# Ordering the engines of a two-layer encoder trunk by a simulation with timelines

## The chip, the core and the metric

The kernel runs on one core of one Trainium2 chip, as one program. The metric is device time in microseconds (us) for one execution; a time without a unit below is in microseconds.

## What is computed

Two layers of an encoder over 256 positions of width 1024, in float32. Each layer is a half step of a gated feed-forward network (FFN, inner width 2816), a mixer, and a second FFN half step:

```
for l in range(DEPTH):
    h_res = h_res + 0.5 * swiglu(rmsnorm(h_res, ffn1_norm[l]), ffn1_w_gate[l], ffn1_w_up[l], ffn1_w_down[l])
    z = rmsnorm(h_res, mix_norm[l]) @ w_in[l]
    zq, zk, zv, zp, hq, hi, hff, hfb, hg = jnp.split(z, split_idx, axis=-1)
    y_att = dilated_attention(zq, zk, zv, q_norm[l], k_norm[l], biases)
    y_pool = pool_mixer(zp, pool_w[l], pool_scale[l])
    y_rec = hgrn2_bidirectional(hq, hi, hff, hfb, hg, lb_all[0, l], lb_all[1, l], hgrn_norm[l])
    h_res = h_res + jnp.concatenate([y_att, y_pool, y_rec], axis=-1) @ w_out[l]
    h_res = h_res + 0.5 * swiglu(rmsnorm(h_res, ffn2_norm[l]), ffn2_w_gate[l], ffn2_w_up[l], ffn2_w_down[l])
```

The attention mixes three dilations, the pooling takes means over windows of 2 to 16, and the recurrence (HGRN2) runs in both directions.

## The kernel before, in words

Every product of float32 matrices is made of three matmuls in the fp32r form: each operand is split into a high part, which is the value rounded by a copy on ScalarE (ACT), and a low part, which is the rest, by a subtraction on VectorE (DVE). TensorE (PE) then adds high by high, high by low and low by high into one PSUM bank (lines 174 to 176, or 167 to 169 where the weights are the stationary operand).

The weights come as a list of 328 halves of 128 x 1024 values in the order of use. SyncE (SP) issues their loads (line 133), four buffers deep. Line 149 makes `whi` of a half on ACT, line 151 makes `wlo` on DVE, or on GpSimd (POOL) for 35 halves of the mixers. Five buffers of each hold what is ready ahead of PE.

The program has six stages: FFN, mixer, FFN in each layer.

- An FFN stage runs over 11 blocks of 256 inner columns. `gate_up` makes 48 matmuls of 512 columns into two `gu` banks; line 345 (ACT, Silu) and line 346 (DVE) make the block's `h`; `turn` transposes it (`hp`, line 352, four transposes) and line 259 (ACT) and line 260 (DVE) split it into `hi` and `lo`; `down` makes 24 matmuls into four `ya` banks, which add up over all blocks. The transposes of a block are traced in the middle of the `down` of the block before.
- A mixer stage projects into `ga`, `gb`, `hq`, `q`, `k`, `zh`, `hg`, `v`, and runs the three head groups between these projections, in the order of a string (`ORDER`). The recurrence goes by levels 0, 1, 2, 4 up to 128: for each level DVE multiplies `U` and `W` (line 520), PE makes a group of small `lev` matmuls (line 541; 549 and 553 for the last two), and DVE or ACT copies the result into place (line 566 and others). The output projection goes to four `wo` banks.
- Between two stages the residual `x` is brought up to date and transposed. There are five such boundaries. The last block's `down` is traced with a hook behind each of the four accumulators:

```
    def add(self, y, by, dh, tt, post):
        s = self.x[:, tt, dh * 512:dh * 512 + 512]
        self.nc.vector.scalar_tensor_tensor(s, y, by, s, op0=ALU.mult, op1=ALU.add)
        post(dh, tt)
```

The add is line 371 (DVE). The hook (`to_stage`) calls `squares` (line 283, ACT, sums of squares for the norm; behind the fourth one an ACT table load, line 287, where the stage needs it) and `turn` (line 296, PE, four transposes into `xps`). When both position halves of a group are there, `parts` makes `xh` (line 274, ACT) and `xl` (line 275, DVE), the split operand of the next stage, in eight pieces numbered k = 0 to 7. One `xps` bank holds two pieces.

The PSUM pool `pg` has four banks, and `gu`, `hp`, `xps`, `ga`, `gb` and most of the mixer's results take turns in them (`self.pg = pool("pg", 4, space=PSUM)`); `py` has four more, for `ya`, `wo` and `lev`. So the first bank that a new stage needs comes free when both pieces of an `xps` bank have been read by line 274 and by line 275.

At the start x comes in transposed, in four pieces (line 114), and as it is (line 119, 1 MB, on ACT's queue). The first weight half is split in two parts, and ACT has in this order: `whi` of the first part, `xh` of pieces 0 and 1, `whi` of the second part, `xh` of pieces 2 to 7, two whole `whi`, the four squares, the table load.

**What sets the order.** The kernel is written with a tile layer. Its scheduler takes the traced operations with their dependencies, a priority by place in the trace, and a simulation of the machine, and writes for each engine a fixed list of instructions with semaphore waits. On the chip each engine goes through its list in that order. SP alone is left in traced order (`manual_schedule`). `keep_in_program_order` and `issue_after` (lines 287, 307, 395) tie a few ACT instructions to others.

## Time and profile before

| | |
|---|---|
| three runs | 1040.72, 1041.35, 1043.30; median 1041.35 |
| the profiled execution | 1040.81, of which 1039.0 is the span of the instructions |
| mean granted PE clock over the span | 0.993 of full speed |
| PE busy | 1004.4 (97%) |
| DVE, ACT, POOL busy | 585.0, 538.8, 88.3 |
| HBM read | 180.2 MB, 176 GB/s over the span |

The profile is of one execution, recorded in hardware. A busy time is the union of an engine's instructions; PE's matmuls overlap each other, since one begins before the one ahead of it has drained, so an idle time of PE below is what is left between the drained and the next. The granted clock is 1.0 where PE runs at 2.4 GHz and 0.5 where it runs at 1.2 GHz. A wait is put down to the instruction whose semaphore came last.

### The profile page before, as it was taken

The numbers are of one execution on the slowest core, as the hardware profiler recorded it, in microseconds if no ns is written. First come the engines' busy times: TensorE is split into PE (matmuls) and PEld (weight loads), VectorE is DVE, ScalarE is ACT, GpSimd is POOL, SyncE is SP. The second block draws the span as 40 slices with busy tenths as digits, with TensorE's granted clock in tenths as the row PEclk, the third lists the DMA queues.
The fourth block names the chain that finished last, engine by engine and source line by source line (L and its number), as shares of the span: only waits on it lengthen the run. The fifth ranks groups of instructions, "written<-read, shape, count | busy, mean of one in ns | idle before, by whom it ended". The sixth has DMA issues, their size and how long they took to land.

```text
span 1039.0 us, 14421 instructions
## 1 busy us (share of the span) xinstructions
PE 1004.4 (97%) x5682; PEld 826.2 (80%) x5682; DVE 585.0 (56%) x776; ACT 538.8 (52%) x774; POOL 88.3 (8%) x43
## 2 busy tenths in 40 slices
PE   6999999998999999999999999999889999999998
PEld 4878888886867888888878888889768678888886
DVE  5655555669835555555565555554977155555553
ACT  7544444684865544444564444447648555444442
POOL 0000000140230000000000000004132400000000
PEclk9999999999999999999999999999989999999999
DMA  7769655553334555555555555554523346555551
GB/s 265 245 219 329 234 188 193 165 163 123 103 122 136 179 192 182 186 192 188 185 168 187 190 185 186 195 185 138 165 83 102 102 147 196 184 185 189 194 186 58
DMA packets 50420, 182.20 MB, mean 175 GB/s; under 512 B 5768, under 2 KB 6024, under 8 KB 49968
## 3 DMA queue, kind: packets, MB, share of 16 engines
q1 hardware_dynamic: 48528, 174.09, 51.6%
q0 software_dynamic: 720, 4.21, 1.1%
q10 hardware_dynamic: 1104, 2.99, 0.8%
q8 instruction: 44, 0.72, 0.3%
q14 instruction: 24, 0.20, 0.1%
HBM read 180.20 MB, written 3.16 MB: 176 GB/s over the span
## 4 chain that ended last, share of the span: by engine, by line
PE 87%; DVE 6%; ACT 3%; issue 3%; DMA 1%; POOL 0%; SPq 0%; ACTq 0%; DVEq 0%; POOLq 0%
PE gu L175 15%; PE gu L176 15%; PE gu L174 15%; PE ya L174 8%; PE ya L176 8%; PE ya L175 8%; PE hp L352 2%; PE wo L174 2%; PE wo L175 1%; PE wo L176 1%; ACT whi L149 1%; DVE wlo L151 1%; PE xps L296 1%; DMA bias<-x_t 1%; PE lev L541 1%
## 5 line engine op out<-in xcount | busy, mean ns | idle before, releaser
L149 ACT ACTIVATE whi<-stage 128x1024 fp32r<-128x1024 f32 (+1 forms) x329 | 347.1, 1056 | 395.3 <-PE gu L176 202.3
L151 DVE TENSOR_TENSOR wlo<-stage,whi 128x1024 fp32r<-128x1024 f32 (+1 forms) x294 | 360.7, 1229 | 337.5 <-ACT whi L149 337.4
L174 PE MATMUL gu<-whi,xh 128*128 128x512 f32 x704 | 275.7, 392 | 8.0 <-ACT xh L274 5.7
L175 PE MATMUL gu<-wlo,xh 128*128 128x512 f32 x704 | 274.9, 391 | 0.5 <-DVE wlo L151 0.5
L176 PE MATMUL gu<-whi,xl 128*128 128x512 f32 x704 | 274.7, 390 | 0.0
L174 PEld LDWEIGHTS gu<-whi,xh 128*128 128x128 f32 x704 | 132.5, 188 | 37.5 <-ACT xh L274 5.7
L175 PEld LDWEIGHTS gu<-wlo,xh 128*128 128x128 f32 x704 | 132.7, 189 | 28.7 <-DVE wlo L151 1.4
L176 PEld LDWEIGHTS gu<-whi,xl 128*128 128x128 f32 x704 | 132.6, 188 | 27.7
L174 PE MATMUL ya<-whi,hi 128*128 128x512 f32 x352 | 141.2, 401 | 0.0
L151 POOL TENSOR_TENSOR wlo<-stage,whi 128x1024 fp32r<-128x1024 f32 x35 | 85.0, 2437 | 654.5 <-ACT whi L149 639.2
L176 PE MATMUL ya<-whi,lo 128*128 128x512 f32 x352 | 137.8, 391 | 0.0
L175 PE MATMUL ya<-wlo,hi 128*128 128x512 f32 x352 | 137.4, 390 | 0.0
L176 PEld LDWEIGHTS ya<-whi,lo 128*128 128x128 f32 x352 | 66.1, 188 | 14.3
L175 PEld LDWEIGHTS ya<-wlo,hi 128*128 128x128 f32 x352 | 66.3, 188 | 12.4
L174 PEld LDWEIGHTS ya<-whi,hi 128*128 128x128 f32 x352 | 66.2, 188 | 12.3
L345 ACT ACTIVATE g<-gu,rc 128x256 f32<-128x256 f32 x88 | 41.5, 475 | 47.4 <-PE gu L176 47.4
L346 DVE SCALAR_TENSOR_TENSOR h<-gu,rc,g 128x256 f32<-128x256 f32 x88 | 42.0, 481 | 23.7 <-ACT g L345 23.7
L260 DVE TENSOR_TENSOR lo<-hp,hi 128x512 fp32r<-128x512 f32 x44 | 30.1, 684 | 2.8 <-ACT hi L259 2.8
L259 ACT ACTIVATE hi<-hp 128x512 fp32r<-128x512 f32 x44 | 25.6, 581 | 2.7 <-PE hp L352 2.7
L541 PE MATMUL lev<-U,W 64*64 64x64 f32 x384 | 15.6, 237 | 11.4 <-DVE W L520 11.4
L352 PEld LDWEIGHTS hp<-cst,h 128*128 128x128 f32 x176 | 21.8, 139 | 5.7
L352 PE MATMUL hp<-cst,h 128*128 128x128 f32 x176 | 26.3, 272 | 0.0
(224 smaller groups left out, 1035.8 us busy)
## 6 DMA issues: line engine op xcount, KB each, us to landing
stage<-w_all SPq DMA_DIRECT2D x327, 512.0 KB, 3.5
skew<-drow POOLq DMA_DIRECT2D x1, 2048.0 KB, 12.1
bias<-skew POOLq DMA_DIRECT2D x2, 1024.0 KB, 10.3
bias<-x_t SPq DMA_DIRECT2D x4, 256.0 KB, 7.9
x<-x ACTq DMA_DIRECT2D x1, 1024.0 KB, 8.4
band<-band ACTq DMA_DIRECT2D x1, 1024.0 KB, 8.0
y_t<-x SPq DMA_DIRECT2D x4, 256.0 KB, 2.2
stage<-w_all SPq DMA_DIRECT2D x2, 256.0 KB, 4.7
```

Of the source, the lines that this page charges most:

```text
L149: nc.scalar.activation(hi[:, s], st[:, s], AF.Copy)
L151: eng.tensor_tensor(lo[:, s], st[:, s], hi[:, s].bitcast(F32), op=ALU.subtract)
L174: nc.tensor.matmul(out, lhsT=ah, rhs=wh, start=start, stop=False, skip_group_check=True)
L175: nc.tensor.matmul(out, lhsT=ah, rhs=wl, start=False, stop=False, skip_group_check=True)
L176: nc.tensor.matmul(out, lhsT=al, rhs=wh, start=False, stop=stop, skip_group_check=True)
L259: self.nc.scalar.activation(hi, src, AF.Copy)
L260: self.nc.vector.tensor_tensor(lo, src, hi.bitcast(F32), op=ALU.subtract)
L296: nc.tensor.transpose(self.xps[k // 2][:, j % 2, tt * P:tt * P + P], self.x[:, tt, k * P:k * P + P], self.ident)
L345: silu = nc.scalar.activation(g2[:, tt, :], gu[tt][:, 0:256], AF.Silu, scale=r)
L346: nc.vector.scalar_tensor_tensor(h[:, tt, :], gu[tt][:, 256:512], r, g2[:, tt, :], op0=ALU.mult, op1=ALU.mult)
L352: nc.tensor.transpose(hp[:, f, tt * P:tt * P + P], h[:, tt, f * P:f * P + P], self.ident)
L541: nc.tensor.matmul(ps[d][e * 64:e * 64 + 64, hb * 64:hb * 64 + 64], lhsT=a, rhs=c, start=(hb == 0), stop=(hb == 7), skip_group_check=True)
```

## The change

One argument is given to the tile layer. Its scheduler then orders the instructions by another simulation of the machine, one that keeps a timeline for each engine, in place of the one it used; the traced operations, their dependencies, the buffers and the kernel's text are otherwise the same.

```diff
-    with tile.TileContext(nc) as tc:
+    with tile.TileContext(nc, schedule_with_timeline_sim=True) as tc:
         trunk_kernel(tc, *args)
```

The lists of PE, DVE and ACT change all through the program; those of SP and POOL stand as they were. No instruction is added or taken away. Three places follow, each as the list stood and as it stands now (line, operation, output and inputs, shape of the output, how many in a row).

**ACT at the start.** `whi` is a weight half's high part, `xh` the split input, `sq` the squares of x, `rc` the norm's factor. Before:

```order
L149 ACTIVATE whi<-stage 128x512
L274 ACTIVATE xh<-bias,prm 128x256 x2
L149 ACTIVATE whi<-stage 128x512
L274 ACTIVATE xh<-bias,prm 128x256 x6
L149 ACTIVATE whi<-stage 128x1024 x2
L283 ACTIVATE sq,ss<-x 128x512 x4
L287 ACT_TABLE_LOAD
```

Now:

```order
L149 ACTIVATE whi<-stage 128x512
L274 ACTIVATE xh<-bias,prm 128x256 x2
L283 ACTIVATE sq,ss<-x 128x512 x4
L287 ACT_TABLE_LOAD
L149 ACTIVATE whi<-stage 128x512
L274 ACTIVATE xh<-bias,prm 128x256 x4
L307 ACTIVATE rc<-rc,cols 128x2
L274 ACTIVATE xh<-bias,prm 128x256 x2
L149 ACTIVATE whi<-stage 128x1024 x2
```

The four squares and the table load now stand ahead of the second part of the first weight half, of six of the eight pieces and of the first whole half.

**PE at the boundary between the layers** (the last `down` of layer 0, then the first `gate_up` of layer 1). `ya` are the four accumulators of `down`, `xps` the transposes of x, `gu` the next stage's first products. Before, the end of it:

```order
L174 MATMUL ya<-whi,hi 128x512
L296 MATMUL xps<-cst,x 128x128 x4
L175 MATMUL ya<-wlo,hi 128x512
L176 MATMUL ya<-whi,lo 128x512
L296 MATMUL xps<-cst,x 128x128 x4
L174 MATMUL gu<-whi,xh 128x512
```

Now:

```order
L176 MATMUL ya<-whi,lo 128x512 x2
L174 MATMUL ya<-whi,hi 128x512
L175 MATMUL ya<-wlo,hi 128x512
L176 MATMUL ya<-whi,lo 128x512
L296 MATMUL xps<-cst,x 128x128 x16
L174 MATMUL gu<-whi,xh 128x512
```

Before, four transposes, one `ya` matmul, four transposes and seven `ya` matmuls stood ahead of these rows, with the third and the last four as shown. Now all sixteen stand behind the last `ya` or `wo` matmul, and so at all five boundaries, and the four accumulators are finished four matmuls apart. In the same stretch the last block's `hp` transposes, which stood twelve `ya` matmuls ahead of the first one that reads their split, now stand one ahead of it, in every FFN stage.

**ACT at the same boundary.** Before:

```order
L149 ACTIVATE whi<-stage 128x1024 x2
L283 ACTIVATE sq,ss<-x 128x512 x2
L274 ACTIVATE xh<-xps,prm 128x256 x2
L283 ACTIVATE sq,ss<-x 128x512
L274 ACTIVATE xh<-xps,prm 128x256 x2
L149 ACTIVATE whi<-stage 128x1024
L283 ACTIVATE sq,ss<-x 128x512
L287 ACT_TABLE_LOAD
L274 ACTIVATE xh<-xps,prm 128x256 x2
```

Now:

```order
L283 ACTIVATE sq,ss<-x 128x512
L149 ACTIVATE whi<-stage 128x1024
L283 ACTIVATE sq,ss<-x 128x512 x2
L149 ACTIVATE whi<-stage 128x1024
L274 ACTIVATE xh<-xps,prm 128x256 x2
L283 ACTIVATE sq,ss<-x 128x512
L287 ACT_TABLE_LOAD
L274 ACTIVATE xh<-xps,prm 128x256 x4
```

All four squares now stand ahead of the table load and of six of the eight `xh`; the pieces come in the order 0, 2, 4, 6, 1, and so on, so the first `xps` bank, with pieces 0 and 1, is free after the fifth. At the boundaries into the second FFN of each layer there is no table load.

In the mixers PE's list moves too. Between one `lev` group and the next, layer 0 had 12 matmuls of 512 columns nearly everywhere. It now has 28, 18, 33 and 15 of them, then one place with 17 score matmuls and four transposes alone, then one with 24 matmuls of 256 columns and 8 score matmuls; layer 1 is alike. The `q` projection is finished before the first `lev` group. In the output projection five `pv` matmuls (256 columns), which stood between the second `hss` and the `wo` that reads the recurrence's result, now stand ahead of that `hss`.

## Rows read from the trace of the kernel before

**Rows 1.** The page, part 1: busy time, share of the span, instructions.

```profile
PE 1004.4 (97%) x5682; PEld 826.2 (80%) x5682; DVE 585.0 (56%) x776; ACT 538.8 (52%) x774; POOL 88.3 (8%) x43
```

**Rows 2.** Stretches of 40 us: busy time of each engine, granted PE clock, DMA.

```profile
400.00:440.00 40.00, 40.00 (x182) 33.11 (x181) 21.09 (x22) 17.97 (x21) 0.00 (x0) 1.00 0.59 190
720.00:760.00 40.00, 36.60 (x398) 30.91 (x401) 32.61 (x43) 25.11 (x34) 12.45 (x5) 0.96 0.51 163
760.00:800.00 40.00, 35.42 (x438) 29.34 (x432) 30.47 (x75) 24.99 (x57) 13.71 (x6) 0.91 0.27 89
800.00:840.00 40.00, 37.53 (x190) 28.76 (x188) 10.53 (x19) 20.97 (x34) 15.27 (x7) 0.96 0.35 110
```

**Rows 3.** Waits of PE: us in total, times, longest.

```profile
PE lev L541 <- DVE W L520: 11.4, 5, 4.5
...
PE wo L174 <- ACT hi L259: 4.5, 2, 2.2
PE xps L296 <- DVE x L371: 3.7, 5, 0.8
...
PE bps L405 <- DMA rel<-rel: 0.7, 1, 0.7
```

**Rows 4.** Timeline of the start: start, us, engine, line, operation, tiles.

```profile
1.66 0.45 ACTq L119 DMA_DIRECT2D x<-x  x1
...
8.38 0.63 ACT L149 ACTIVATE whi<-stage 128x512 fp32r<-128x512 f32 x1 [2.28 <-DMA stage<-w_all]
...
15.02 0.50 PE L175 MATMUL gu<-wlo,xh 128*128 128x512 f32 x1 [0.53 <-DVE wlo L151]
...
17.36 1.28 ACT L287 ACT_TABLE_LOAD   x1
```

**Rows 5.** The page, part 6: KB each, median us from issue to landing.

```profile
x<-x ACTq DMA_DIRECT2D x1, 1024.0 KB, 8.4
```

**Rows 6.** Timeline of PE at the boundary between the layers.

```profile
521.03 0.66 PE L296 MATMUL xps<-cst,x 128*128 128x128 f32 x4 [0.78 <-DVE x L371]
521.44 0.48 PE L174 MATMUL gu<-whi,xh 128*128 128x512 f32 x1
521.76 0.39 PE L175 MATMUL gu<-wlo,xh 128*128 128x512 f32 x1
521.99 0.40 PE L176 MATMUL gu<-whi,xl 128*128 128x512 f32 x1
```

**Rows 7.** Timeline of ACT at the same boundary.

```profile
516.06 1.06 ACT L149 ACTIVATE whi<-stage 128x1024 fp32r<-128x1024 f32 x1 [1.66 <-PE ya L176]
517.02 0.62 ACT L283 ACTIVATE sq<-x 128x512 f32<-128x512 f32 x1
...
518.25 0.81 ACT L274 ACTIVATE xh<-xps,prm 128x256 fp32r<-128x256 f32 x2
```

**Rows 8.** Groups by line, shapes apart: busy us, mean ns of one, idle before.

```profile
L151 DVE TENSOR_TENSOR wlo<-stage,whi 128x1024 fp32r<-128x1024 f32 x292 | 359.3, 1232 | 335.0 <-ACT whi L149 335.0
...
L352 PE MATMUL hp<-cst,h 128*128 128x128 f32 x176 | 26.3, 272 | 0.0
L259 ACT ACTIVATE hi<-hp 128x512 fp32r<-128x512 f32 x44 | 25.6, 581 | 2.7 <-PE hp L352 2.7
...
L275 DVE SCALAR_TENSOR_TENSOR xl<-xps,prm,xh 128x256 fp32r<-128x256 f32 x40 | 17.6, 478 | 1.3 <-ACT xh L274 1.0
...
L566 DVE COPY_PREDICATED A<-msk,lev 128x512 f32<-128x512 uint8 x20 | 14.7, 734 | 0.7 <-PE lev L541 0.5
...
L520 DVE TENSOR_TENSOR U<-U,dw 128x512 f32<-128x512 f32 x14 | 13.4, 960 | 0.1
...
L371 DVE SCALAR_TENSOR_TENSOR x<-ya,x 128x512 f32<-128x512 f32 x16 | 10.8, 688 | 10.1 <-PE ya L176 10.1
```

**Rows 9.** Short stretches of the mixers: busy time, granted PE clock.

```profile
306.00:311.00 5.00, 2.63 (x14) 1.56 (x15) 2.21 (x4) 2.70 (x5) 2.31 (x1) 1.00 0.65 202
746.00:750.00 4.00, 3.29 (x68) 2.95 (x69) 3.94 (x7) 0.99 (x2) 0.00 (x0) 0.57 0.36 130
```

## The prediction

> **What bounds it now.** I read the page's busy times first: PE is busy for 1004.4 of 1039.0 [rows 1]. Then stretches of 40 us: inside an FFN stage PE is busy for all 40.00, with DVE and ACT at about half [rows 2]; only in the mixers does it fall to 35 to 38. So PE's own work is nearly the whole time, it is the same work after the change, and what an order can move is PE's idle time and its clock. Of idle time the table of PE's waits is short [rows 3]: 11.4 in five waits of the `lev` groups for DVE's `W`, 4.5 in two waits of `wo`, 3.7 in five waits at the stage boundaries, 0.7 at the bias setup. To these come the start, until matmuls run dense at about 15 [rows 4], and the stretches at the lower clock, below. There is thus little to win, some 20 in all, and a great deal of well covered work to uncover.
>
> The sum is made against the profiled execution, 1040.8, which lies 0.5 under the median of the runs.
>
> **The start.** Before, ACT splits the second part of the first half at 8.38, and PE reads the first whole low half at 15.02 [rows 4]. Now the four squares stand first, and they need x, which is issued at 1.66 and takes 8.4 to land [rows 4, 5]: 10.06. Four squares at 0.62 [rows 7] end at 12.54, the table load of 1.28 [rows 4] at 13.82, the part of 0.63 at 14.45, six `xh` at half of 0.81 [rows 7] at 16.9, the whole half of 1.06 [rows 7] at 18.0, its low half of 1.23 [rows 8] at 19.2. That is 4.2 later than 15.02. PE can meanwhile run two more high-part matmuls of 0.23 (the step between two starts in [rows 6]), and the setup's DMAs are issued earlier, so that I let the 0.7 of the bias setup [rows 3] go: **+3.0**. The ends are +2 (some of the delayed work finds DMA waits that it would have met anyway) and +4.2. Nothing recovers this later, since PE is dense until the first boundary.
>
> **The five boundaries** carry most of the sum. Before, eight or twelve of the sixteen transposes run between `ya` matmuls, `xh` and `xl` of the first pieces are made while PE still works on the stage before, and PE idles 0.78 for the last add, once per boundary [rows 3, 6]. Now all transposes stand behind the last `ya`. I work out the new wait from the moment at which the first accumulator's last matmul is issued.
>
> PE's side: the other three accumulators take 12 matmuls, at 0.23 between two starts 2.8; sixteen transposes, at four in 0.41 (521.03 to the next matmul at 521.44 [rows 6]), take 1.6. PE has 4.4 of work.
>
> The other side: the matmul drains 0.17 beyond its step (0.40 less 0.23 [rows 6]), the add takes 0.69 [rows 8]. Then ACT in its new order, with the steps of [rows 7]: a square 0.62, a `whi` 0.96 (516.06 to 517.02), two squares 1.24, a `whi` 0.96, two `xh` 0.81, the last square 0.62, the table load 1.28 [rows 4], and three more `xh` 1.20, for the first `xps` bank is free after the fifth piece: 7.7. Then `xl` of that piece, 0.48 [rows 8]. Together 9.0, and PE idles 9.0 - 4.4 = 4.6. That holds for the boundaries into layer 0's mixer, into layer 1 and into its mixer; at the first of these, small operations for the recurrence's lower bounds stand between as well, which I leave to the upper end. At the two boundaries into a second FFN there is no table load: 3.3. The sum is 3 x 4.6 + 2 x 3.3 = 20.4, less the 3.7 of before: **+16.7**. Lower end: if PE's first product waited for the first piece alone, four `xh` and, where it stands, the table load drop out, some 2.4 each, and +5 remains; the four banks of `pg` speak against that, for the sixteen transposes hold all of them. Upper end: +22, with 1 us for each boundary of waits among DVE, ACT and PE that I have not counted.
>
> **The last block of each FFN.** Before, twelve `ya` matmuls cover the split of `hp`. Now one of 0.23 does. The last transpose takes 0.27, the split on ACT 0.58 [rows 8]: PE waits 0.27 + 0.58 - 0.23 = 0.6, four times, **+2.5**; at the least 0, if the list lets the split begin with the first transposes.
>
> **The mixers.** Before, 12 matmuls at 0.23 cover 2.8 of a level's work on DVE, which has `U` and `W` (0.96 for `U`, and I take `W` alike), two masked copies of 0.73, and often a `wlo` of 1.23 [rows 8]: 3.4 to 4.6. That is why PE waits. With 28, 18, 33 and 15 matmuls, 3.5 to 7.6, the level is covered, and the 11.4 [rows 3] go. What is late next is the level behind 17 score matmuls and four transposes: at the transposes' 0.10 these cover 2.1 of the 3.4, a wait of 1.3. I take two such per layer, 5.2 in all (bounds 0 and 11.4: none, or as much as before). At `wo` the five `pv` matmuls no longer cover the recurrence's chain: 256 columns are half of a step of 0.23 at the least and a whole one at the most, so 0.6 to 1.2 per layer; I take 1.0 and so 2.0. Net **-4.2**, between -10 and +2.
>
> **The clock.** In three of the stretches of [rows 2] the granted clock is 0.96, 0.91 and 0.96 instead of 1.00. With 1.2 and 2.4 GHz as the two levels that is 3.2, 7.2 and 3.2 us at the lower one, 13.6 in all, at which PE does half the work: 6.8 lost at the most. In [rows 9] the 0.57 of 746 to 750 comes right behind one of the five `lev` waits; but 306 to 311, which holds a `wo` wait of 2.2, stays at 1.00. Seven waits of this size and three falls; a fall cost 2.3. The new program has seven waits over 3: the five boundaries and the two of `wo` (2.2 and 1.0). I take four falls, 9.1, so **+2.3**; the ends are none (-6.8) and one for each (+9.3). The Trainium skill ("TensorE: Matmul & The Clock Gate", section "HAM oscillation — how this bites in real kernels") says that a kernel which waits between its groups of matmuls pays the return of the lower clock at each such group, not once. Here the trace agrees with it in three cases of seven; by the rule the term would be the upper end, +9.3, and the sum 1068.
>
> **Sum.** 3.0 + 16.7 + 2.5 - 4.2 + 2.3 = +20.3, so 1040.8 + 20.3 = 1061.
>
> **The rivals.**
>
> *A fall of the clock behind every long wait.* The boundaries' waits are longer than most of the old ones, and the longest old one (4.5) stood in the stretch with 7.2 at the lower level. Against it: four of seven did without. 1061 + 7 = 1068.
>
> *A small wait in every FFN block.* DVE's and ACT's lists change there as well; 44 blocks at the 0.27 of one transpose would give +12, 1073. Against it: PE is 40.00 of 40.00 with both engines half idle [rows 2], and the splits stand several halves ahead.
>
> *Not slower: the boundaries are covered after all.* The place is the first product behind the transposes. If it needs only what ACT makes before the last squares and the table load, PE idles 9.0 - 4.4 less 0.6, 1.3, 1.2 and a `whi` of 1.0: 0.5 instead of 4.6. The point from which it decides is a wait of about 0.75 per boundary, what is paid now. Then the boundaries give -1, and with the `lev` waits gone without new ones, and no clock falls: 1040.8 + 3.0 - 1 + 2.5 - 9.4 - 6.8 = 1029. For it speaks that half of ACT's time is idle [rows 1]; against it, that the rows at this place are a chain and not a load, and that all four banks are held.
>
> *The lists differ and the time does not.* Gains in the mixers (-10) and at the clock (-6.8) could meet the start and boundaries at their lower ends (+2, +5) and the blocks' 2.5 or so: 1034 to 1045. For it: PE's work is the same and the old list has 20 of waits to give.
>
> **How the numbers follow.** My forecast has 0.66, with a range of its own of 1050 to 1067. The clock rival has 0.14, the block rival 0.06, the covered boundaries 0.05, the equal time 0.09, of which I put a third each below, within and above no change. About 0.3%, 3.1 us, is what a measurement of this kernel can tell from no change. Faster: 0.05 + 0.03 = 0.08. Same: 0.03, and 0.03 from the foot of my own case if most terms lie at their lower ends: 0.06. Slower: the rest, 0.86. For 8 in 10 the range takes in my own case and the clock's: 1047 to 1071; it leaves out the block rival, the covered boundaries and most of the equal time.
>
> **What would show it.** PE's waits should list, for the first product of each stage (`ga`, `gu`), a wait for DVE's `xl` of 3 to 5, five times, in place of `xps` for the add; `lev` for `W` should fall from 11.4 to under 7 and `wo` for `hi` rise from 4.5 to about 6.5; four waits of `ya` for `hi` of about 0.6 should be new. At the start ACT's second part should stand near 14.5. The five boundaries' timelines would show the chain `xh`, square, table load, `xh`, `xl` with PE idle. The forecast is wrong if the boundaries' waits stay under 1, if the `lev` waits do not fall, or if new waits stand inside the FFN blocks.

## The result, and the profile after

The changed kernel takes 1076.9 us (median; 1075.3 to 1077.9) beside 1042.3 (1040.7 to 1043.3) before: a ratio of 1.0332, 95% interval 1.0311 to 1.0353. The forecast was 1061, 1047 to 1071. The direction was right, the size was not: 34.6 us slower instead of 20, and outside the range. The profiled execution spans 1073.5, 34.5 more than before.

PE does the same work and is busy for a little longer [rows 1]. Page of the kernel after, part 1:

```profile
PE 1018.2 (95%) x5682; PEld 837.0 (78%) x5682; DVE 593.8 (55%) x776; ACT 537.8 (50%) x774; POOL 89.7 (8%) x43
```

PE is busy for 13.8 more with the same 5682 matmuls, so part of them ran slower; the other 20.7 are idle time. Waits of PE, kernel after (us in total, times, longest); these rows answer to [rows 3]:

```profile
PE gu L174 <- DVE xl L275: 10.0, 3, 4.1
PE ga L167 <- DVE xl L275: 9.1, 2, 5.0
PE wo L174 <- ACT hi L259: 7.3, 2, 3.7
PE gu L174 <- ACT xh L274: 6.1, 1, 6.1
PE gu L174 <- ACT whi L149: 5.6, 2, 5.0
PE tp L660 <- DVE zq L651: 4.9, 3, 2.8
PE lev L541 <- DVE W L520: 2.5, 2, 1.5
PE ya L174 <- ACT hi L259: 1.8, 4, 0.5
PE tp L660 <- DVE zk L651: 1.7, 1, 1.7
PE lev L541 <- ACT zq L641: 1.1, 1, 1.1
PE xps L296 <- DVE x L371: 0.6, 2, 0.3
```

The five boundaries now wait 19.1 for `xl`. The `lev` groups, 11.4 before, are at 2.5. New, and in no term of the prediction, are 6.6 us in which the transposes of the mixer (`tp`) wait for DVE's scaling of `zq` and `zk`.

The clock is the second half of the story. Stretches of the kernel after (busy time of PE, PEld, DVE, ACT and POOL, granted PE clock, DMA share, GB/s):

```profile
206.00:211.00 5.00, 0.10 (x1) 0.00 (x0) 4.20 (x12) 4.97 (x14) 2.83 (x2) 0.89 0.53 159
211.00:216.00 5.00, 4.88 (x23) 4.88 (x24) 2.33 (x13) 0.85 (x4) 0.00 (x0) 0.50 0.14 54
...
780.00:783.00 3.00, 0.32 (x24) 0.18 (x13) 3.00 (x2) 0.13 (x1) 2.34 (x1) 1.00 0.48 164
783.00:787.00 4.00, 3.49 (x11) 2.80 (x12) 3.51 (x7) 0.47 (x1) 0.00 (x0) 0.57 0.46 143
...
544.00:548.00 4.00, 4.00 (x11) 3.12 (x11) 0.73 (x2) 0.28 (x2) 0.00 (x0) 0.52 0.00 0
```

PE stands still in the first and third row and works at about the lower of the two levels in the row behind each; the last row lies behind the wait of 4.07 at the boundary between the layers. A "fall" is a stretch that the trace records at the lower level, each 3.4 or 6.8 us long. After the start the trace holds eight such falls, 37.5 us long together, with PE busy for 31.1 of them; before there were three, with 11.8 busy. At half speed the difference costs up to (31.1 - 11.8) / 2 = 9.7. With the start's part, up to 2.7 (below), that makes 12.4 of the 13.8 by which PE's busy time grew.

By stage (the first from the span's start, each from the end of the fourth add into x to that of the next; the wait for `xl` counts to the stage behind the boundary, the wait for the last add to the one ahead of it), worked out from the two traces: length, PE idle, and PE's busy time at the lower level, the start's included:

| stage | before: length, idle, low | after: length, idle, low | longer by |
|---|---|---|---|
| layer 0, FFN 1 | 201.3, 9.9, 5.1 | 205.1, 12.1, 10.5 | 3.8 |
| layer 0, mixer | 131.9, 7.8, 0.0 | 140.7, 12.1, 9.0 | 8.8 |
| layer 0, FFN 2 | 187.8, 0.8, 0.0 | 193.0, 3.7, 3.4 | 5.2 |
| layer 1, FFN 1 | 188.1, 0.6, 0.0 | 194.4, 4.8, 4.3 | 6.3 |
| layer 1, mixer | 140.1, 11.2, 11.8 | 144.7, 14.9, 10.9 | 4.6 |
| layer 1, FFN 2 | 186.3, 0.1, 0.0 | 192.1, 3.4, 3.4 | 5.8 |

Every stage is longer, the three FFN stages behind a boundary by 5 to 6 each. The boundary into layer 1's mixer, in the timeline of the kernel after:

```profile
733.41 0.81 ACT L274 ACTIVATE xh<-xps,prm 128x256 fp32r<-128x256 f32 x2
734.13 0.62 ACT L283 ACTIVATE sq<-x 128x512 f32<-128x512 f32 x1
...
734.86 1.28 ACT L287 ACT_TABLE_LOAD   x1
736.15 1.57 ACT L274 ACTIVATE xh<-xps,prm 128x256 fp32r<-128x256 f32 x4
...
736.66 2.52 DVE L275 SCALAR_TENSOR_TENSOR xl<-xps,prm,xh 128x256 fp32r<-128x256 f32 x6 [1.04 <-ACT xh L274]
...
737.98 0.58 PE L167 MATMUL ga<-xh,whi 128*128 128x256 f32 x1 [4.08 <-DVE xl L275]
```

This is the chain of the prediction, link by link: two `xh`, the last square, the table load, more `xh`, then `xl`, and PE waits 4.08 where 4.6 was worked out.

### The profile page after: what moved, and what is told of

Its sections match the earlier page's. It is cut to its first block, busy times and chain, and to the rows that moved or that the text cites. A ratio compares the mean times of both kernels' runs of the same rounds, so it can differ in the third digit from the quotient of the medians.

```text
span 1073.5 us, 14417 instructions
## 1 busy us (share of the span) xinstructions
PE 1018.2 (95%) x5682; PEld 837.0 (78%) x5682; DVE 593.8 (55%) x776; ACT 537.8 (50%) x774; POOL 89.7 (8%) x43
## 4 chain that ended last, share of the span: by engine, by line
PE 86%; DVE 7%; ACT 4%; issue 2%; DMA 1%; ACTq 0%; DVEq 0%
PE gu L174 15%; PE gu L175 15%; PE gu L176 15%; PE ya L174 7%; PE ya L175 7%; PE ya L176 7%; PE hp L352 2%; PE wo L174 2%; PE wo L175 1%; PE wo L176 1%; ACT whi L149 1%; DVE wlo L151 1%; ACT sq L283 1%; PE pv L721 1%; DVE xl L275 1%
## 5 line engine op out<-in xcount | busy, mean ns | idle before, releaser
L174 PE MATMUL gu<-whi,xh 128*128 128x512 f32 x704 | 278.6, 397 | 21.6 <-DVE xl L275 10.0
L175 PE MATMUL gu<-wlo,xh 128*128 128x512 f32 x704 | 278.4, 395 | 0.0
L176 PE MATMUL ya<-whi,lo 128*128 128x512 f32 x352 | 140.6, 409 | 0.0
L174 PE MATMUL ya<-whi,hi 128*128 128x512 f32 x352 | 137.7, 391 | 1.8 <-ACT hi L259 1.8
L175 PEld LDWEIGHTS ya<-wlo,hi 128*128 128x128 f32 x352 | 66.1, 188 | 13.8
L352 PE MATMUL hp<-cst,h 128*128 128x128 f32 x176 | 33.0, 272 | 0.0
L174 PE MATMUL wo<-whi,hi 128*128 128x512 f32 x48 | 19.7, 410 | 7.3 <-ACT hi L259 7.3
## 6 DMA issues: line engine op xcount, KB each, us to landing
skew<-drow POOLq DMA_DIRECT2D x1, 2048.0 KB, 12.1
```

Of the source, the lines that this page charges most:

```text
L174: nc.tensor.matmul(out, lhsT=ah, rhs=wh, start=start, stop=False, skip_group_check=True)
L175: nc.tensor.matmul(out, lhsT=ah, rhs=wl, start=False, stop=False, skip_group_check=True)
L176: nc.tensor.matmul(out, lhsT=al, rhs=wh, start=False, stop=stop, skip_group_check=True)
L352: nc.tensor.transpose(hp[:, f, tt * P:tt * P + P], h[:, tt, f * P:f * P + P], self.ident)
```

## The experiments

Times are medians beside runs of the kernel before on the same chip (1042.3 to 1043.6). "Idle" is PE's idle time in the profiled execution, from its first matmul to its last, "low" its busy time at the lower level after the start, "falls" how often the clock fell after the start.

| kernel | us | ratio to before (95%) | idle | low | falls |
|---|---|---|---|---|---|
| before | 1042.3 | 1 | 24.6 | 11.8 | 3 |
| after | 1076.9 | 1.0332 (1.0311 to 1.0353) | 45.0 | 31.1 | 8 |
| e1, after, spare work in the boundaries | 1074.2 | 1.0300 (1.0279 to 1.0321) | 30.1 | 20.3 | 5 |
| e2, after, turns put back | 1062.9 | 1.0183 (1.0155 to 1.0211) | 33.6 | 32.2 | 7 |
| e3, before, turns behind | 1062.2 | 1.0177 (1.0148 to 1.0207) | 37.7 | 34.3 | 8 |
| e4, after, start put back | 1074.4 | 1.0301 (1.0280 to 1.0322) | 42.3 | 35.8 | 9 |
| e5, e2 and e4 | 1053.1 | 1.0109 (1.0091 to 1.0126) | 28.1 | 20.9 | 5 |
| e6, after, four splits from POOL to DVE | 1071.5 | 1.0280 (1.0260 to 1.0300) | 39.6 | 39.8 | 9 |
| e7, before, two splits from POOL to DVE | 1037.4 | 0.9954 (0.9936 to 0.9971) | 22.2 | 3.4 | 1 |
| e8, before, spare work in two waits | 1040.2 | 0.9979 (0.9967 to 0.9991) | 18.7 | 13.6 | 4 |
| e9, e5 and e6 | 1050.4 | 1.0067 (1.0050 to 1.0084) | 22.1 | 26.0 | 5 |
| e10, before, four splits from POOL to DVE | 1033.6 | 0.9908 (0.9891 to 0.9924) | 18.4 | 6.6 | 2 |

**e3: the boundary alone, in the old lists.**

```diff
             if (dh, tt) == (1, 1):
-                self.pending = lambda: self.turn(stage, dh, tt)
-            else:
-                self.turn(stage, dh, tt)
+                for a in range(2):
+                    for b in range(2):
+                        self.turn(stage, a, b)
```

> The kernel before, with its own scheduler, and only the sixteen transposes of a boundary written behind the last accumulator: the boundary part of the change by itself; start, FFN blocks and mixers stay as they were. Theory A: PE waits 2 to 4.5 us at each of the five boundaries (10 to 20 in all, less the 3.7 of now), and the clock falls behind most of them: 1052 to 1066. Rival (the boundary is not what costs, the mixers and the start are): within 4 us of 1042.

Measured: 1062.2, 19 over the kernel before, inside theory A. Its waits of PE:

```profile
PE gu L174 <- DVE xl L275: 9.6, 3, 4.2
PE ga L167 <- DVE xl L275: 7.7, 2, 4.2
```

17.3 of waits in place of 3.7, with no other part of the change: away from the boundaries all lists stand as before. The falls rose from three to eight. So the sixteen transposes behind the last `ya` are enough for more than half of the loss, by the wait and by the clock together.

**e2: the boundary taken out of the new lists.** Each accumulator's transposes are written behind the next one's matmuls, and these are tied behind them:

```diff
+                with self.tc.issue_after(self.tie.ins) if post is not None and self.tie is not None else nullcontext():
...
+            self.turns.append(lambda: self.turn(stage, dh, tt))
...
+                self.turns.pop(0)()
+                self.pending, self.tie = self.turns.pop(0), None
+            elif len(self.turns) > 1:
+                self.turns.pop(0)()
```

> The changed kernel, with the transposes of a finished accumulator tied between the matmuls of the accumulators that follow, as the list of the kernel before has them. Theory A (the transposes that all stand behind the last ya are what the boundaries cost): the five waits for xl, 19.1 together, fall to 3 to 6, the clock's falls behind them (at most 13.6 lost) go as well, and the time is 1048 to 1056. Rival (ACT's and DVE's lists at the boundary set it, not PE's; or the loss lies in the mixers): PE waits as long, now elsewhere at the boundary, and the time stays above 1066.

```profile
PE xps L298 <- DVE x L373: 3.0, 7, 0.6
...
PE gu L175 <- DVE xl L277: 1.3, 1, 1.3
PE ga L168 <- DVE xl L277: 1.3, 1, 1.3
```

The waits did what theory A said (2.6 for `xl` left of 19.1, and 3.0 for the adds), the time only half of it: 1062.9 instead of 1048 to 1056. The low time did not fall (32.2 after 31.1): of the five boundary falls three went, two boundaries kept one, behind waits of only 1.3, and five falls stood behind mixer waits of 1.5 to 3.7. So a short wait at a boundary does not rule out a fall behind it. And e2's lists moved in a few other places as well: a `lev` group of layer 1 has 19 `hg` products ahead of it, where the kernel after has 24 and five score matmuls, and waits 1.80, where that kernel does not wait.

**e1: the waits filled with work.**

```diff
-                self.pending = lambda: self.turn(stage, dh, tt)
+                self.pending = lambda: (self.turn(stage, dh, tt), self.fill(14 if stage % 3 == 2 else 20))
...
+        for j in range(n):
+            self.nc.tensor.matmul(out.rearrange("p (a t) -> p a t", a=4), lhsT=self.bones, rhs=rhs, start=(j == 0), stop=(j == n - 1),
+                                  skip_group_check=True)
```

> The changed kernel, with 14 to 20 spare products of 512 columns behind the last turn of each of the five boundaries; nothing reads their result, they only keep PE at work where it now waits for xl. Theory A (the wait itself makes the clock fall behind it): the wait of the next stage's first product turns into spare work, the boundaries end as late as now, and of the eight stretches at the lower clock those that follow a boundary go. Five of the eight lie there (at 209.9, 349.9, 541.0, 735.6 and 882.3 us, 6.8 + 3.4 + 6.8 + 6.8 + 3.4 = 27.3 us at half speed, so at most 13.6 lost): the time falls by 7 to 13, to 1064 to 1070. Theory B (the falls are not due to the waits, or cost next to nothing because what follows waits for other engines anyway): the time stays within 3 us of 1077, or rises by the spare work that sticks out.

Stretches of e1, at the first boundary and in layer 0's mixer:

```profile
206.00:211.00 5.00, 4.78 (x27) 3.69 (x26) 3.75 (x9) 4.49 (x13) 2.94 (x2) 1.00 0.54 160
211.00:216.00 5.00, 3.59 (x30) 3.60 (x31) 3.15 (x15) 1.61 (x5) 0.00 (x0) 1.00 0.13 50
...
282.00:286.00 4.00, 4.00 (x19) 3.78 (x18) 4.00 (x16) 3.69 (x14) 0.00 (x0) 0.50 0.02 6
```

With PE at work through the boundary the clock stays at 1.00 where it was 0.50; all five boundary falls are gone. Waiting is what the clock falls behind. But the time is only 2.7 lower, inside theory B's range, while the boundary falls went as theory A had it: three falls came new behind mixer waits of 2.4, 2.2 and 1.5, one went, and 88 products at about 0.23 are 20 us of work for 15 of idle time removed. The wait of 2.2 is new as well: in this list a `lev` group of layer 1 has seven `hg` products just ahead of it instead of ten. As a price of the falls the run is inconclusive.

**e4: the start alone.**

```diff
-        nc.scalar.activation(hi[:, s], st[:, s], AF.Copy)
+        self.last_hi = nc.scalar.activation(hi[:, s], st[:, s], AF.Copy)
...
-        for dh in range(2):
-            for tt in range(2):
-                self.squares(0, dh, tt)
+        with self.tc.issue_after(self.last_hi.ins):
+            for dh in range(2):
+                for tt in range(2):
+                    self.squares(0, dh, tt)
```

> The changed kernel, with ACT's four squares at the start tied behind the splits of the first weights, as ACT's list stands in the kernel before. Theory A (the squares, which wait for x, hold up the first splits, and nothing gives this back later): the second block's first product starts at about 20.7 instead of 25.9 us and the time falls by 4 to 5, to 1072 to 1073. Rival (the start is given back at the first boundary, or the DMA of the weights sets it): within 1.5 us of 1077.

The first stage ends at 200.3 instead of 205.1, 4.8 earlier, as expected; the time is only 2.5 lower, short of theory A's 4 to 5, since the next stage got 2.5 longer with 4.6 more low time. In the start of the kernel after:

```profile
12.01 1.28 ACT L287 ACT_TABLE_LOAD   x1
13.30 0.63 ACT L149 ACTIVATE whi<-stage 128x512 fp32r<-128x512 f32 x1
...
13.98 1.22 PE L174 MATMUL gu<-whi,xh 128*128 128x512 f32 x2 [4.99 <-ACT whi L149]
...
21.50 0.63 PE L176 MATMUL gu<-whi,xl 128*128 128x512 f32 x1
...
22.28 0.40 PE L175 MATMUL gu<-wlo,xh 128*128 128x512 f32 x1
```

ACT's second part stands at 13.30 (8.38 before, [rows 4]) and PE stops for 4.99. Only at 22 does a matmul take 0.40 instead of 0.63; before, that came at 12.5:

```profile
12.09 0.61 PE L174 MATMUL gu<-whi,xh 128*128 128x512 f32 x1
12.52 0.42 PE L175 MATMUL gu<-wlo,xh 128*128 128x512 f32 x1
```

The prediction's start had the wait and not this.

**e6: the new waits in the mixers.** In the kernel after:

```profile
780.20 2.34 POOL L151 TENSOR_TENSOR wlo<-stage,whi 128x1024 fp32r<-128x1024 f32 x1 [10.20 <-ACT whi L149]
...
780.25 3.44 DVE L651 TENSOR_TENSOR zq<-zq,hs 128x512 f32<-128x512 f32 x2
...
783.15 0.33 PE L660 MATMUL tp<-cst,zq 128*128 128x128 f32 x1 [2.83 <-DVE zq L651]
```

Two operations that take 1.29 elsewhere take 3.44. POOL's split beside them ends at 782.54, and they end at 783.69, 1.15 later, as if they had stood still until then. e6 changes two tuples and leaves PE's and ACT's lists as they are:

```diff
-POOL_HALVES = ((3, 4, 5, 7, 8, 9, 12, 16, 20, ...), (2, 5, 6, 7, 8, 12, 16, 18, 19, 20, 21, ...))
+POOL_HALVES = ((3, 4, 5, 7, 8, 9, 12, 20, ...), (2, 5, 6, 7, 8, 12, 18, 21, ...))
```

> The changed kernel with four of its 35 POOL splits given to DVE (half 16 of both layers' mixers, halves 19 and 20 of layer 1); PE's and ACT's lists stay as they are. In the trace of the changed kernel DVE's scaling of zq at 780.25 takes 3.44 us for two operations instead of 1.29, and that of zk 2.1 longer, each beside a POOL split of 2.4. Theory A (a DVE operation with two operands in SBUF stands still while POOL splits, and that is what PE's new waits for zq and zk consist of): these DVE operations fall back to 0.68 each, PE's waits of tp for zq and zk from 6.6 to under 3, and the time falls by 3 to 8. Rival (DVE is simply late there, and 1.23 more per half makes it later): the waits stay or grow, and the time is within 2 of 1077 or above it.

```profile
780.43 1.28 DVE L651 TENSOR_TENSOR zq<-zq,hs 128x512 f32<-128x512 f32 x2
...
781.17 0.33 PE L660 MATMUL tp<-cst,zq 128*128 128x128 f32 x1 [0.70 <-DVE zq L651]
```

The two operations are back at 1.28, the `tp` waits at 1.1 of 6.6, and the time is 5.4 lower although DVE has four splits more and the clock fell nine times. The collision is the cause of these waits.

**e7 and e10: the same in the kernel before.** There the longest `lev` wait of [rows 3] stands behind the same thing:

```profile
762.67 2.37 POOL L151 TENSOR_TENSOR wlo<-stage,whi 128x1024 fp32r<-128x1024 f32 x1 [6.89 <-ACT whi L149]
765.44 2.35 POOL L151 TENSOR_TENSOR wlo<-stage,whi 128x1024 fp32r<-128x1024 f32 x1 [0.40 <-ACT whi L149]
...
763.75 1.85 DVE L520 TENSOR_TENSOR U<-U,dw 128x512 f32<-128x512 f32 x1
765.52 2.82 DVE L520 TENSOR_TENSOR W<-W,dw 128x512 f32<-128x512 f32 x1
...
768.49 0.37 PE L541 MATMUL lev<-U,W 64*64 64x64 f32 x2 [4.55 <-DVE W L520]
```

The edit takes halves 18 and 19 out of layer 1's tuple in e7, and half 12 out of both besides in e10.

> The kernel before, with two of its POOL splits given to DVE (halves 18 and 19 of layer 1's mixer), the ones beside which U took 1.85 and W 2.82 us instead of 0.68. Theory A (the longest lev wait, 4.5, is made of this collision): that wait falls to 1 to 3, the clock's fall of 6.8 behind it shrinks or goes, and the time is 1036 to 1041. Rival (DVE's two extra splits of 1.23 take what the collision gives back): within 2 of 1042.5.

> The kernel before, with half 12 of both mixers on DVE beside halves 18 and 19 of layer 1: the POOL splits beside which DVE's W of the first level took 3.31 and 3.46 us instead of 1.22 are gone too. Theory A (the collision costs DVE 2.1, the split itself 1.23, so W of the next level comes 0.9 earlier in each layer): the lev waits of 2.3 and 2.5 fall to about 1.4, and the time is 1 to 3 under the 1037.4 of the two halves alone. Rival (DVE's own list is the longer one here): 1037 or more.

Timeline of e7:

```profile
764.96 0.68 DVE L520 TENSOR_TENSOR U<-U,dw 128x512 f32<-128x512 f32 x1
765.55 0.69 DVE L520 TENSOR_TENSOR W<-W,dw 128x512 f32<-128x512 f32 x1
...
766.39 0.27 PE L541 MATMUL lev<-U,W 64*64 64x64 f32 x2 [1.87 <-DVE W L520]
```

The wait fell from 4.55 to 1.87 and the fall behind it went: 1037.4, faster than before. e10 brought the first level's W from 3.31 and 3.46 to 1.22 in both layers; of the two waits behind it the one in layer 0 fell to 1.29, as expected, the one in layer 1 only to 2.16. At 1033.6, 3.8 under e7 where 1 to 3 were expected, e10 beats both kernels, by 0.92% (0.76 to 1.09) the one before.

**e8: spare work in the kernel before.** The `lev` groups of levels 2 and 16 of layer 1 get 10 and 19 products ahead of them:

```diff
+                for j in range({(1, 2): 10, (1, 16): 19}.get((l, m), 0)):
+                    nc.tensor.matmul(ps[0].rearrange("p (a t) -> p a t", a=4), lhsT=self.bones,
+                                     rhs=self.bones[:, None, :].to_broadcast([P, 4, P]), start=True, stop=True, skip_group_check=True)
```

> The kernel before, with 10 and 19 spare products of 512 columns ahead of the two lev groups of layer 1 that wait 2.4 and 4.6 us; they write the bank that the group itself then starts anew, and nothing reads them. DVE's and ACT's lists stay as they are. Theory A (waiting is what makes the clock fall): the falls at 746.4 and 766.9 go (3.4 + 6.8 us at half speed, at most 5.1 lost), and the time falls by 2 to 5. Theory B (the falls come anyway at some point of the mixer, or the spare work costs as much): within 1.5 of 1042.5, or slower.

1040.2, 2.1 lower, the foot of theory A's range. The two falls went, and layer 1's mixer is 3.7 shorter; but layer 0's, where nothing was changed, is 4.4 longer in the profiled execution, which took 1042.3 and was the longest of twelve, with three falls behind waits of 2.3, 1.9 and 2.2 that had none in the first trace.

**e5 and e9: the repairs together.**

> The changed kernel with both earlier repairs at once: transposes back between the accumulators, and the start's squares behind the first splits. What is left of the change are the mixers' lists, the last FFN blocks and the clock. Theory A (start and boundary together are most of the loss, and their shares add): 1077 less 14 less 3 to 5, so 1057 to 1061; of the 15 to 19 that then remain, about 10 stand in layer 1's mixer stage, where waits moved from lev to the transposes of zq and the clock falls behind them. Rival (the two repairs act on the same slack): 1062 or more.

> The changed kernel with all three repairs: transposes between the accumulators, the start's squares behind the first splits, and the four POOL splits on DVE. Theory A (the three are separate losses, which add): 1053 less the 3 to 6 that the POOL splits gave, so 1047 to 1050; what is left over the kernel before is the wo waits (2.8 more), the last FFN blocks (1.8) and the rest of the clock. Rival (the POOL splits' gain came from the clock's scatter): within 1.5 of 1053.

e5 came out lower than either theory, 1053.1: start and boundary did not share slack, and the low time fell to 20.9, which it had not in e2. e9 is at 1050.4, 26.5 under the kernel after, just above theory A. It idles less than the kernel before (22.1 against 24.6), but its two long waits are these:

```profile
PE wo L175 <- ACT hi L261: 7.3, 2, 3.7
```

Each has a fall of 6.83 behind it, and 26.0 low against 11.8 is up to 7.1 of the 10.0 by which its span is the longer. The start's low time (10.9 against 5.1) is up to 2.9 more, the idle time 2.5 less; the remaining 2.5 I could not assign. No run put the cover of `wo` or of the last FFN blocks back: what these cost is read from their waits alone.

**The two kernels once more,** for the chance in the clock:

> The kernel before, unchanged, for a second trace. Theory A (which waits the clock falls behind is chance, with better odds the longer the wait): the falls stand behind other waits than 744.3, 763.9 and 822.5, and their number differs from three by one or two; all waits are as long as they were. Rival (the lists fix the falls): the same three falls at the same places, 13.6 us at half speed.

> The changed kernel, unchanged, for a second trace. Theory A: again seven to ten falls, nearly one behind each of the eight waits of 2.8 and over, but not the same lengths; the half-speed time is within 10 of 37.5. Rival (the eight falls were a bad draw): four to five falls, and the time at half speed near 20.

The kernel after had the same eight falls, with the same lengths. The kernel before had three again, two of them behind the same waits, the third elsewhere; its second trace shows the first row, its first trace the second:

```profile
239.00:243.00 4.00, 4.00 (x56) 3.26 (x45) 3.97 (x7) 0.00 (x0) 0.00 (x0) 0.57 0.27 91
```

```profile
239.00:243.00 4.00, 4.00 (x46) 3.33 (x37) 3.97 (x7) 0.61 (x1) 0.00 (x0) 1.00 0.31 83
```

The same list, the same wait of about 2.2 just ahead, and once a fall and once none. Of all 14 traces together, with each fall after the start counted to the longest wait ahead of it: of 50 waits of PE over 2.6, 49 had a fall behind them; of 60 between 1.2 and 2.6, 27; of 43 between 0.7 and 1.2, one. The bounds of these groups were chosen on the same traces, and many of the waits are the same place in several kernels, so they are counts of this program and no law. For long waits e11's rival holds (the lists fix the falls), and e12's eight were no bad draw; for waits of about 2 e11's theory A holds (chance).

## Why the prediction was wrong

| term | predicted | measured | from |
|---|---|---|---|
| start | +3.0 | +4.8 | first stage, after against e4 |
| five boundaries | +16.7 | +16.0 | 19.1 + 0.6 less 3.7 |
| last FFN blocks | +2.5 | +1.8 | `ya` for `hi` |
| mixers | -4.2 | +0.4 | `lev` 12.3 to 3.6, `tp` 0.3 to 6.6, `wo` +2.8 |
| clock | +2.3 | up to +9.7 | low time 11.8 to 31.1 |
| sum | +20.3 | +32.7 of 34.5 | 1.8 not assigned |

The mixers' row takes in two waits of the kernel before beside those of [rows 3]:

```profile
PE lev L541 <- DVE W L510: 0.9, 1, 0.9
...
PE tp L660 <- DVE st L695: 0.3, 1, 0.3
```

**Right:** the boundaries, by chain, place and size; the last blocks; `wo` at 7.3 (6.5 forecast); that the `lev` waits go; and that no wait appears inside the FFN blocks, which refutes that rival. The covered boundaries (1029) and the equal time are refuted by the 19.1.

**The step that failed most is the clock's:** "Seven waits of this size and three falls ... I take four falls". It took +2.3 where up to +9.7 came. Six of the seven were of that size; one of the `lev` waits was 0.23. It threw waits of 1.9 to 2.5, of which here about half are followed by a fall, together with the one of 4.5, and then applied their odds to five waits that the same text had worked out as 3.3 and 4.6. All eight waits of 2.8 and over had their fall, in both traces. The rival with a fall behind every long wait, +9.3, had this term right (up to 9.7); its 1068 fell short by the other terms. The sentence of the Trainium skill beside it ("TensorE: Matmul & The Clock Gate", section "HAM oscillation — how this bites in real kernels"), that the return of the lower clock is paid at each group of matmuls that had to wait, agrees with these traces for the long waits (49 of 50) and not for those between 1.2 and 2.6 (27 of 60).

**The second is in the mixers.** The gain was there, larger than forecast (`lev` -8.7 where -6.2 was taken). What the step left out is POOL: it costed DVE's operations at their means in the old order, and asked only which of them would be late next for the `lev` groups. The new list sets the scaling of `zq` and `zk` beside POOL's splits, and PE waits for them directly. The rows stood in the trace of before: `U` at a mean of 960 ns [rows 8] is 0.68 in most cases and 1.2 to 1.9 in a few, and a mean hid it.

**The third is the start:** the wait was 4.99, where 3.0 was left after savings, and the clock's first rise came 9.6 us later, up to 2.7 of lost time (10.5 against 5.1 us of low time in the first stage, halved), for which the prediction had no term. Against the kernel before and not e4, PE's 700th matmul, still in the first stage, starts 4.5 later.

## What to carry to other kernels

Where PE is the bound, price a wait of its queue together with what the clock does behind it, and count waits by length: one of 4 us here cost 4 us and up to 3.4 more, five of up to 0.8 cost 3.7 in all. Before a list is reordered, look on the timeline for what POOL does beside each DVE operation on the new path, and read the longest case of a group, not its mean. Handing two to four splits from POOL to DVE made either list's kernel faster by 5 to 10 us here, and e9 faster than e5 by 2.7.

## What the runs showed of the hardware

A DVE operation with two operands in SBUF that began beside a running split of POOL stood still for the rest of it: `zq` 2.17 longer, `W` 2.14, `zk` 5.03 for two beside two splits in a row (5.33). Two kinds that read PSUM kept their time beside a split of POOL: in the 14 traces `xl` took 0.47 to 0.49 in all 34 cases, the masked copies 0.72 to 0.76 in all 41. And it works the other way: where DVE's split had begun, POOL's next to it took 3.35 instead of 2.40. In the kernel after:

```profile
267.69 1.22 DVE L151 TENSOR_TENSOR wlo<-stage,whi 128x1024 fp32r<-128x1024 f32 x1
...
267.80 3.35 POOL L151 TENSOR_TENSOR wlo<-stage,whi 128x1024 fp32r<-128x1024 f32 x1 [13.67 <-DVE zk L651]
```

The Trainium skill ("SBUF — State Buffer", section "SBUF: two separate sides") has this as an exclusive lock that the later operation waits out; the traces agree.

Whether the clock falls behind a wait of about 2 us differed between executions of one list: e7's eleven runs spread from 1033.1, at a mean granted clock of 0.999, to 1041.4, at 0.992. At the start the granted clock of the profile's stretches reads 1.00 while matmuls still take 0.63 instead of 0.40, so the lower level has to be read from durations there.
